# A hybrid decoder block on one core: 448 instead of 384 tokens of the expert mixer are gathered, the first value rows come beside the recurrence, and three transposes move behind the first dots

## The chip, the cores and the metric

The kernel runs on one core of one Trainium2 chip. The metric is the device time of one execution in microseconds (us), lower is better; one execution in each set is also recorded by the hardware profiler.

## What is computed

For 1024 tokens of width 1024 the block projects its modulated input, runs an RWKV-7 recurrence and a top-k attention beside each other, merges the two with gates, and then applies PEER, an expert mixer with product keys. PEER is the part that the change touches:

```python
# q, keys1, keys2: per head the 16 best of 128 keys on each side, then the 16 best of the 256 sums
idx  = i1 * 128 + i2                  # 8 heads x 16 slots = 128 experts of 16384 for every token
gate = softmax(scores)                # over the 16 slots of a head
h    = gelu(einsum('td,tkd->tk', h2, u[idx]))   # 128 dots of 1024 for a token
y    = einsum('tk,tkd->td', gate * h, v[idx])
out  = layer_norm(alpha * x + mod * y)
```

## The kernel before, in words

The projection, the recurrence and the attention run in two halves H of 512 tokens each (H=0, then H=1). In each half `rwkv` and `attn` are staggered, then `merge` writes what PEER needs. Beside `rwkv` of H=1 the first gathered rows of PEER are worked on, since the first half's tokens are known by then.

PEER is done in two ways, by token:

- **Gathered** (the first `NG` = 3 tiles of 128 tokens). For each of the 128 slots of a tile one indirect DMA fetches the u row that each token chose (128 partitions x 1024 floats, 0.524 MB), and VectorE takes its dot with the token (L1389). For each slot a second one fetches the v row, which VectorE multiplies by the gated dot and adds to the sum `pg` (L1391, L1393). The DMAs are issued by POOL (L1385, into tiles `g`, `gx`, `g2`). A "row" below is one such DMA with its VectorE operation: 256 for each tile, 768 in all, numbered from 0. Rows 0 to 7 have no due place; rows 8 to `ROW1` are tied to places in the recurrence of H=1 (56 "anchors" on VectorE, L699 and L763: the row's VectorE operation is placed no sooner than its anchor, `behind` at L1336); rows `EARLY` to `MIDDLE` go beside the table stage, the rest beside the dense stage. Rows below `EARLY` have three buffers (`g`, GB); between `EARLY` and `MIDDLE` three more (`gx`); after that `g` and one `g2`.
- **Dense** (the other `DN` = 640 tokens). All 128 blocks of u and all 128 of v (128 rows each) stream through TensorE for all these tokens. A block is loaded as `raw` by SP (L1267), rounded to `whi` by ACT (L232), and its rest `wlo` is taken by POOL (L1271, `split2`). `mm6` (L1281) then issues, for each of 8 chunks, six matmuls of 128 x `DN`/2 columns (L1284, L1286, L1288): 48 of 320 columns for a block. 69 of the u blocks are done ahead in the table stage (`dots_ahead`, into `dotD`), the others in `dense_u` (L1301); v blocks are in `dense_v` (L1319), whose last group of 8 is streamed twice, once for 384 and once for 256 columns, so 264 blocks are split in all. The gates of these tokens are first written out as tables over all experts (`gate_table`, L1240): 16 chunks of 8 tokens for each 128 tokens, each with two comparisons on VectorE and 8 matmuls in 16 passes of TensorE (L1258).

`retrieve` (L1118) finds keys and gates for a tile of tokens; `by_slot` (L1228) transposes them on TensorE (L1233) for the table. Tiles 1 to 3 are retrieved beside the merge of H=1, tiles 4 to 7 in the table stage. Tile 3 is the first dense one. `finish` (L1424) scales a gathered tile's sum, adds the residual and normalises (`out_rows`, L1400); `fin1` (L1445) does the same for dense tokens after the last group.

A tile scheduler fixes the order of the instructions on each engine when the program is built; on the chip each engine works through its own list in that order. POOL's list holds both the `wlo` splits and the issues of the gather DMAs; an issue whose buffer is not yet free holds whatever stands behind it.

## Time and profile before

| | us |
|---|---|
| three runs | 3740.57, 3749.42, 3751.53 (median 3749.42) |
| the profiled execution: its own time | 3743.65 |
| its span in the profile | 3741.9 |
| PE busy | 3505.2 (94%) |
| VectorE (DVE) busy | 2596.4 (69%) |
| POOL busy | 1981.3 (53%) |
| ACT busy | 1695.7 (45%) |
| mean granted TensorE clock | 0.967 of full speed |

The parts of the span, in order: projection, recurrence and attention of H=0, its merge (about 780 us), the recurrence of H=1 with the first gathered rows (1018 to 1440 us), its merge (to 1643), the table stage (1643 to 2380), the dense stage (2380 to 3593), and the last 149 us, in which the last 24 of the 264 blocks are split. PE is TensorE's matmuls, DVE is VectorE, ACT is ScalarE, POOL is GpSimd, SP is SyncE. The rows of the trace that the prediction uses stand in a section of their own below. A PE row with "x2" is two passes that the trace shows together; every shown time is from the start of the span.

### The profile page before, as it was taken

How to read it: one execution, taken by the hardware profiler on the slowest of the kernel's cores; microseconds unless marked ns; L12 is line 12 of the kernel's file. 1: busy time of each engine (PE TensorE's matmuls, PEld its weight loads, DVE VectorE, ACT ScalarE, POOL GpSimd, SP SyncE). 2: the span in 40 equal slices, each digit the busy share in tenths (PEclk: the TensorE clock that was granted, in tenths of full speed). 3: DMA queues.
4: the chain of work that ended last, by engine and by line, in shares of the span. 5: the costliest groups of instructions: out<-in, count | busy, mean ns of one | idle time of the engine just before them, and what ended most of it. 6: DMA issues, size and time to landing. Idle time of an engine off the chain costs nothing.

```text
span 3741.9 us, 64784 instructions
## 1 busy us (share of the span) xinstructions
PE 3505.2 (94%) x24045; PEld 3139.0 (84%) x24045; DVE 2596.4 (69%) x5433; ACT 1695.7 (45%) x3230; POOL 1981.3 (53%) x1572
## 2 busy tenths in 40 slices
PE   8999999889999999869999999999999999999997
PEld 7677777666677777649999989999999999999997
DVE  7756653857467775899999985376777767676754
ACT  3549953243344443447667678322223322222223
POOL 5452222354455553245655532467677667677755
PEclk9999999989999999889999999999999999999998
DMA  7463323864676666378988864898999989989963
GB/s 231 137 171 103 107 87 123 290 196 161 214 220 219 215 212 218 115 250 317 335 308 316 309 240 171 292 333 322 334 330 331 323 319 327 340 320 325 333 225 123
DMA packets 436880, 920.95 MB, mean 246 GB/s; under 512 B 36452, under 2 KB 195508, under 8 KB 433876
## 3 DMA queue, kind: packets, MB, share of 16 engines
q1 hardware_dynamic: 311956, 498.38, 39.8%
q0 software_dynamic: 124608, 418.43, 31.4%
q8 instruction: 189, 3.10, 0.3%
q14 instruction: 127, 1.04, 0.1%
HBM read 791.59 MB, written 125.08 MB: 245 GB/s over the span
## 4 chain that ended last, share of the span: by engine, by line
PE 49%; DVE 14%; DMA 13%; issue 8%; POOL 7%; ACT 6%; SPq 0%; POOLq 0%; ACTq 0%; DVEq 0%
PE pair L1284 7%; PE pair L1286 7%; PE pair L1288 7%; PE acc L423 4%; PE acc L424 4%; PE acc L425 4%; POOL g L1385 3%; DMA g<-in_u_dram,gidx 3%; DMA raw<-in_vt_dram 3%; POOL wlo L1271 3%; DMA g<-in_v_dram,gidx 3%; PE tp L1258 2%; DMA raw<-in_ut_dram 2%; ACT gt L232 2%; PE acc L975 2%
## 5 line engine op out<-in xcount | busy, mean ns | idle before, releaser
L1271 POOL TENSOR_TENSOR wlo<-raw,whi 128x1024 fp32r<-128x1024 f32 x264 | 643.8, 2440 | 388.9 <-ACT whi L232 367.5
L413 POOL TENSOR_TENSOR wlo<-wraw,whi 128x512 fp32r<-128x512 f32 x280 | 371.3, 1329 | 557.3 <-ACT whi L232 505.9
L232 ACT ACTIVATE whi<-raw 128x1024 fp32r<-128x1024 f32 x264 | 278.9, 1057 | 681.1 <-PE pair L1286 320.7
L1385 POOL DMA_INDIRECT g<-in_u_dram,gidx x361 | 373.6, 1035 | 298.4 <-DVE g L1389 180.5
L1284 PE MATMUL pair<-A,whi 128*128 128x320 f32 (+2 forms) x2048 | 482.1, 312 | 25.6 <-DVE A L1316 18.3
L1393 DVE SCALAR_TENSOR_TENSOR pg<-g,dots,pg 128x1024 f32<-128x1024 f32 x317 | 407.1, 1284 | 123.1 <-DMA g<-in_v_dram,gidx 118.0
L1286 PE MATMUL pair<-A,whi 128*128 128x320 f32 (+2 forms) x2048 | 481.2, 311 | 0.2 <-DVE A L1316 0.2
L1288 PE MATMUL pair<-A,wlo 128*128 128x320 f32 (+2 forms) x2048 | 480.4, 311 | 0.6 <-POOL wlo L1271 0.6
L1288 PE MATMUL pair<-h2T,wlo 128*128 128x320 f32 x2048 | 474.3, 312 | 2.1 <-POOL wlo L1271 2.1
L1284 PE MATMUL pair<-h2T,whi 128*128 128x320 f32 x2048 | 475.6, 312 | 0.2 <-ACT ds L232 0.2
L1286 PE MATMUL pair<-h2T,whi 128*128 128x320 f32 x2048 | 473.3, 311 | 0.0
L1385 POOL DMA_INDIRECT g<-in_v_dram,gidx x320 | 307.7, 961 | 170.8 <-DVE pg L1393 80.8
L423 PE MATMUL acc<-big,whi 128*128 128x512 f32 x864 | 356.5, 413 | 18.6 <-DVE zs L531 6.8
L1284 PEld LDWEIGHTS pair<-A,whi 128*128 128x128 f32 x2048 | 349.1, 190 | 28.2 <-issue 19.1
L1389 DVE SCALAR_TENSOR_TENSOR g<-g,pg 128x1024 f32<-128x1024 f32 x233 | 281.0, 1216 | 118.4 <-DMA g<-in_u_dram,gidx 116.8
L425 PE MATMUL acc<-big,wlo 128*128 128x512 f32 x864 | 351.6, 407 | 2.3 <-POOL wlo L413 2.3
L424 PE MATMUL acc<-big,whi 128*128 128x512 f32 x864 | 349.5, 404 | 3.1 <-DVE big L449 3.1
L1288 PEld LDWEIGHTS pair<-A,wlo 128*128 128x128 f32 x2048 | 349.1, 190 | 0.8 <-POOL wlo L1271 0.8
L1286 PEld LDWEIGHTS pair<-A,whi 128*128 128x128 f32 x2048 | 349.2, 190 | 0.7 <-DVE A L1316 0.7
L1288 PEld LDWEIGHTS pair<-h2T,wlo 128*128 128x128 f32 x2048 | 343.8, 189 | 3.5 <-POOL wlo L1271 2.6
L1284 PEld LDWEIGHTS pair<-h2T,whi 128*128 128x128 f32 x2048 | 344.6, 189 | 1.6 <-ACT ds L232 0.4
L1286 PEld LDWEIGHTS pair<-h2T,whi 128*128 128x128 f32 x2048 | 343.9, 189 | 1.0
(482 smaller groups left out, 6682.5 us busy)
## 6 DMA issues: line engine op xcount, KB each, us to landing
raw<-in_vt_dram SPq DMA_DIRECT2D x136, 512.0 KB
raw<-in_ut_dram SPq DMA_DIRECT2D x128, 512.0 KB
gtD<-st SPq DMA_DIRECT2D x20, 2048.0 KB
gt<-gtD SPq DMA_DIRECT2D x32, 1280.0 KB
wraw<-in_wz_dram SPq DMA_DIRECT2D x152, 256.0 KB
dotD<-ds SPq DMA_DIRECT2D x69, 320.0 KB
al<-dotD SPq DMA_DIRECT2D x69, 320.0 KB
mw<-in_wada_dram SPq DMA_DIRECT2D x32, 512.0 KB
```

The source lines that it names most:

```text
L232: copy = lambda o, i, **k: A.activation(o, i, AF.Copy, **k)
L413: G.tensor_tensor(lo, raw, hi.bitcast(F32), op=OP.subtract)
L423: mm(pt, lhsT=wh[:, ks], rhs=ah[:, k, :], start=k == 0, stop=False)
L424: mm(pt, lhsT=wh[:, ks], rhs=al[:, k, :], start=False, stop=False)
L425: ins = mm(pt, lhsT=wl[:, ks], rhs=ah[:, k, :], start=False, stop=k == nk - 1)
L1271: G.tensor_tensor(lo, raw, hi.bitcast(F32), op=OP.subtract)
L1284: mm(pts[n], lhsT=wh, rhs=ah[:, h], start=k == 0, stop=False)
L1286: mm(pts[n], lhsT=wh, rhs=al[:, h], start=False, stop=False)
L1288: mm(pts[n], lhsT=wl, rhs=ah[:, h], start=False, stop=last)
L1385: G.indirect_dma_start(out=u, out_offset=None, in_=a["u" if n < 2 else "v"], in_offset=bass.IndirectOffsetOnAxis(ap=idx[:, k:k + 1], axis=0))
L1389: V.scalar_tensor_tensor(u, u, 1.0, h2, op0=OP.mult, op1=OP.mult, accum_out=dots[:, k:k + 1])
L1393: V.scalar_tensor_tensor(acc, u, dots[:, k:k + 1], acc, op0=OP.mult, op1=OP.add)
```

## The change

A fourth, smaller tile of 64 tokens (`GX`) is gathered, so `DN` falls from 640 to 576 and a matmul of `mm6` from 320 to 288 columns; the last group is split 384 + 192. The small tile is packed: partitions 0 to 63 carry slots 0 to 63 of its 64 tokens, partitions 64 to 127 slots 64 to 127, so it takes 64 u rows and 64 v rows, each still 128 x 1024. Its two halves are added by two matmuls with a matrix `sel` in `finish`. Its index, gates and token rows come by two SP DMAs each (`rows_in`); one more tile of `xaD` and `h2D` is written in the merge of H=0 (one DVE and one POOL product of 128 x 1024 for each, two SP DMAs). The gate table of tile 3 has 8 chunks instead of 16.

Rows up to 192 instead of 128 are tied to the recurrence of H=1: the first tile's first 64 value rows are now among them. They are summed in SBUF (`gacc`) and copied once to PSUM at row 192. `MIDDLE` moves from 300 to 364, so that 172 rows stay beside the table stage. The name `GX` of before, the three extra buffers, is now `XR`.

Tile 3's `by_slots` (three transposes and the copies behind them) no longer stands ahead of the table stage: it comes after the first three blocks of dots (`FIRST`), tied behind the last matmul of the third.

```diff
-EARLY = 128
+EARLY = 192
...
-MIDDLE = 300
+MIDDLE = 364
...
-GX = 3
+FIRST = 3
+XR = 3
...
-ROW1 = 128
+ROW1 = 192
 NG = 3
-TD = NG * 128
+GX = 64
+TD = NG * 128 + GX
+NGT = NG + (GX > 0)
 DN = 1024 - TD
...
-        for tt, xn in enumerate(xns[:max(0, NG - 4 * H)]):
+        for tt, xn in enumerate(xns[:max(0, NGT - 4 * H)]):
...
-        for b in range(16):
+        for b in range(max(0, TD - i * 128) // 8, 16):
...
     def gather_all(at):
-        for i in range(NG):
+        for i in range(NGT):
             acc = yield from peer_gather(i, at)
             finish(i, acc, at)
+    def rows_in(dst, src, n, c):
+        for r in range(128 // n):
+            at = 0 if src.shape[1] == c else r * c
+            nc.sync.dma_start(dst[r * n:r * n + n, 0:c], src[0:n, at:at + c])
     def peer_gather(i, at):
         pg = at["pg"]
+        tokens = 128 if i < NG else GX
+        slots_ = tokens
+        halves = 2 if i < NG else 1
...
-        for n in range(4):
-            half = slice(64 * (n % 2), 64 * (n % 2) + 64)
-            if n == 2:
-                acc = pg.tile([128, 1024], F32, name="pg")
+        for n in range(2 * halves):
+            half = slice(0, slots_) if halves == 1 else slice(64 * (n % 2), 64 * (n % 2) + 64)
+            if n == halves:
+                acc = (gp.tile([128, 1024], F32, name="gacc") if i == 0 and EARLY > 128 else
+                       pg.tile([128, 1024], F32, name="pg"))
...
+                if row == EARLY and EARLY > 128:
+                    so_far, acc = acc, pg.tile([128, 1024], F32, name="pg")
+                    copy(acc, so_far)
...
     def finish(i, acc, at):
+            sel = gp.tile([128, 1024], F32, name="gh2")[:, 0:n]
+            V.tensor_reduce(sel, ident.rearrange("p (s t) -> p t s", t=n), axis=AX.X, op=OP.add)
+            copy(y2, acc)
+            acc = at["pg"].tile([128, 1024], F32, name="pg")
+            for h in range(2):
+                hs = slice(512 * h, 512 * h + 512)
+                mm(acc[p, hs], lhsT=sel, rhs=y2[:, hs], start=True, stop=True)
...
-                side = retrieve_all(range(1, M1), tk, by_slots)
+                side = retrieve_all(range(1, M1), tk, keep)
...
-            for i in slots:
-                table(i)
...
             ahead_ = dots_ahead()
+            for _ in range(FIRST):
+                next(ahead_)
+            for i, f in early_found.items():
+                with tc.issue_after(latest[0].ins):
+                    by_slots(i, f)
+                table(i)
```

In the built program there are 896 rows instead of 768; 169 instead of 118 of them stand between the first and the last anchor in the recurrence of H=1. In the line numbers of the changed kernel the row DMA is L1402, its products L1406 to L1410, `wlo` L1274, the matmuls of `mm6` L1287, L1289 and L1291, the transposes L1236, the end of a gathered tile L1432.

DVE's list in the recurrence of H=1, before (`ST` is the state, `w` a work tile of the recurrence, `g` a gathered row):

```order
L699 TENSOR_TENSOR w<-w,rw 128x256
L1389 SCALAR_TENSOR_TENSOR g,dots<-g,gh_15759 128x1024
L684 TENSOR_TENSOR w<-w,C 128x256
L763 TENSOR_TENSOR ST<-ST,fs 128x128
L1389 SCALAR_TENSOR_TENSOR g,dots<-g,gh_15759 128x1024 x2
L687 STREAM_TRANSPOSE in<-w 128x256 x2
```

and after:

```order
L760 TENSOR_TENSOR ST<-ST,rw 128x128
L1406 SCALAR_TENSOR_TENSOR g,dots<-g,gh_15768 128x1024
L690 STREAM_TRANSPOSE in<-w 128x256
L687 TENSOR_TENSOR w<-w,C 128x256
L960 ISA p,asm<-tp,mask_8226 128x512
L960 ISA asm 128x1
L766 TENSOR_TENSOR ST<-ST,fs 128x128
L1406 SCALAR_TENSOR_TENSOR g,dots<-g,gh_15768 128x1024
```

More rows stand between the same steps of the recurrence and the attention, 169 where there were 118.

PE's list at the start of the table stage, before (L425 is the last matmul of the merge, L1233 the transposes of tile 3, L1128 the keys of the next tile, L1284 and so on the first block of dots):

```order
L425 MATMUL acc<-Q,wlo 128x512
L1233 MATMUL tp<-ident,i_15675 128x128
L1233 MATMUL tp<-ident,gates 128x128
L1233 MATMUL tp<-ident,i_15674 128x128
L1128 MATMUL tp<-keysT,qT 128x128 x4
L1284 MATMUL pair<-h2T,whi 128x320 x2
```

and after, the end of the merge with the first dots:

```order
L428 MATMUL acc<-Q,wlo 128x512
L1287 MATMUL pair<-h2T,whi 128x288 x2
L1289 MATMUL pair<-h2T,whi 128x288 x2
L1287 MATMUL pair<-h2T,whi 128x288 x2
L1289 MATMUL pair<-h2T,whi 128x288 x2
```

and, three blocks of dots on, the place to which the transposes have moved:

```order
L1289 MATMUL pair<-h2T,whi 128x288 x2
L1291 MATMUL pair<-h2T,wlo 128x288 x2
L1236 MATMUL tp<-ident,i_15685 128x128
L1236 MATMUL tp<-ident,gates 128x128
L1236 MATMUL tp<-ident,i_15684 128x128
L1131 MATMUL tp<-keysT,qT 128x128 x2
```

The dots now stand ahead of the transposes on PE.

POOL's list at its end, before (`g` and `g_36500` are the last row DMAs, `wlo` the blocks' splits, L1415 the normalisation of dense rows):

```order
L1271 TENSOR_TENSOR wlo<-raw,whi 128x1024
L1385 DMA g<-in_v_dram,gidx 128x1024 x3
L1385 DMA g_36500<-in_v_dram,gidx 128x1024
L1271 TENSOR_TENSOR wlo<-raw,whi 128x1024 x11
L1415 TENSOR_TENSOR gacc<-gacc,gt 128x512 x2
L1271 TENSOR_TENSOR wlo<-raw,whi 128x1024 x6
```

and after, around the last `wlo` of the program, behind which only rows and the normalisation of the last tiles stand:

```order
L1402 DMA g_36486<-in_u_dram,gidx 128x1024
L1274 TENSOR_TENSOR wlo<-raw,whi 128x1024
L1402 DMA g<-in_u_dram,gidx 128x1024 x3
L1274 TENSOR_TENSOR wlo<-raw,whi 128x1024
L1402 DMA g_36498<-in_u_dram,gidx 128x1024
L1402 DMA g<-in_u_dram,gidx 128x1024 x3
L1402 DMA g_36510<-in_u_dram,gidx 128x1024
L1402 DMA g<-in_u_dram,gidx 128x1024 x3
```

Before, the last row stands ahead of the last 22 splits, and 7 rows stand behind the 240th. After, 137 rows stand behind the 240th split: 52 between it and the last one, and 85 (21 u rows and the 64 v rows of the small tile) behind the last one. Between the 72nd and the 240th split there were 461 rows, 2.74 for each; now there are 395, 2.35 for each.

## Rows read from the trace of the kernel before

**Rows 1.** Busy time by stretch: start:end, length, busy us (count), clock, DMA share, GB/s.

```profile
core 0: us, PE busy (x) PEld busy (x) DVE busy (x) ACT busy (x) POOL busy (x), PEclk, DMA share, GB/s
275.00:643.00 368.00, 354.80 (x3363) 278.92 (x3362) 199.36 (x575) 248.10 (x622) 96.91 (x101) 0.96 0.34 102
1018.00:1440.00 422.00, 388.88 (x3616) 303.54 (x3617) 299.04 (x669) 195.89 (x434) 221.62 (x192) 0.97 0.70 217
1643.00:1677.00 34.00, 2.99 (x16) 1.93 (x15) 28.79 (x64) 10.52 (x14) 19.26 (x17) 0.56 0.91 321
1677.00:2250.00 573.00, 548.13 (x3885) 534.66 (x3886) 523.76 (x1249) 397.23 (x811) 316.66 (x222) 0.99 0.83 300
1800.00:1900.00 100.00, 96.27 (x695) 94.49 (x694) 91.20 (x168) 70.48 (x149) 64.58 (x47) 0.98 0.94 349
2380.00:3593.00 1213.00, 1194.50 (x8073) 1192.10 (x8073) 851.97 (x1042) 340.24 (x419) 838.51 (x628) 0.99 0.91 327
3593.00:3742.00 149.00, 125.86 (x848) 124.72 (x846) 61.47 (x86) 43.14 (x55) 81.48 (x43) 0.93 0.41 138
```

**Rows 2.** The same by stretch, for line 1385 (row DMAs issued by POOL) alone.

```profile
1018.00:1440.00 422.00, 136.75 (x117) 0.97 0.70 217
2380.00:3593.00 1213.00, 435.14 (x461) 0.99 0.91 327
```

**Rows 3.** DVE's waits in the recurrence of H=1: total us, times, longest us.

```profile
DVE g L1389 <- DMA g<-in_u_dram,gidx: 40.4, 34, 3.2
```

**Rows 4.** One piece of the chain that ended last, in the recurrence: start, us.

```profile
1057.32 6.26 DMA g<-in_u_dram,gidx
```

**Rows 5.** Timeline of PE and POOL, start of the table stage: start, us, idle before.

```profile
1674.93 0.45 PE L1233 MATMUL tp<-ident,i 128*128 128x128 f32 x1 [31.01 <-DVE i L1193]
1676.89 0.90 PE L1284 MATMUL pair<-h2T,whi 128*128 128x320 f32 x2
1657.53 4.64 POOL L1271 TENSOR_TENSOR wlo<-raw,whi 128x1024 fp32r<-128x1024 f32 x2
```

**Rows 6.** Timeline of PE: matmuls of 320, 384 and 256 columns in a row.

```profile
2649.97 0.46 PE L1288 MATMUL pair<-h2T,wlo 128*128 128x320 f32 x2
2650.85 0.46 PE L1288 MATMUL pair<-h2T,wlo 128*128 128x320 f32 x2
3659.82 0.33 PE L1288 MATMUL pair<-A,wlo 128*128 128x384 f32 x1
3660.51 0.33 PE L1284 MATMUL pair<-A,whi 128*128 128x384 f32 x1
3702.05 0.29 PE L1284 MATMUL pair<-A,whi 128*128 128x256 f32 x1
3702.54 0.28 PE L1286 MATMUL pair<-A,whi 128*128 128x256 f32 x1
```

**Rows 7.** PE's costliest groups: the passes of the gate tables, busy us, mean ns.

```profile
L1258 PE MATMUL tp<-gt 128*128 128x128 f32 x1280 | 161.7, 279 | 14.2 <-ACT st L232 11.5 <-ACT sc L232 2.5
```

**Rows 8.** Timeline of DVE in the dense stage: first and last of eight products.

```profile
3126.79 1.22 DVE L1389 SCALAR_TENSOR_TENSOR g<-g,pg 128x1024 f32<-128x1024 f32 x1 [3.25 <-DMA g<-in_u_dram,gidx]
3142.36 1.22 DVE L1389 SCALAR_TENSOR_TENSOR g<-g,pg 128x1024 f32<-128x1024 f32 x1
```

**Rows 9.** Timeline of POOL: a split, two row DMAs in a row, the last split.

```profile
3593.11 2.42 POOL L1271 TENSOR_TENSOR wlo<-raw,whi 128x1024 fp32r<-128x1024 f32 x1 [8.85 <-ACT whi L232]
3596.93 0.94 POOL L1385 DMA_INDIRECT g<-in_v_dram,gidx  x1 [0.30 <-issue]
3598.18 0.94 POOL L1385 DMA_INDIRECT g<-in_v_dram,gidx  x1 [0.30 <-issue]
3716.94 4.75 POOL L1271 TENSOR_TENSOR wlo<-raw,whi 128x1024 fp32r<-128x1024 f32 x2 [2.32 <-ACT whi L232]
```

**Rows 10.** Timeline of POOL in the merge of H=0, and of DVE near the end.

```profile
783.39 8.58 POOL L1089 TENSOR_TENSOR xo<-xo,big 128x1024 f32<-128x1024 f32 x2
3725.76 0.48 DVE L1330 SCALAR_TENSOR_TENSOR yacc<-pair,modc,yacc 128x256 f32<-128x256 f32 x1 [2.15 <-PE pair L1288]
```

More of the change, by code (lines that the diff above doesn't have):

```diff
@@ L442, in body @@
         ybD[H] = tc.dram_tile([8, 128, 512], F32, name=f"ybD{H}")
-    xaD = [tc.dram_tile([128, 1024], F32, name=f"xaD{i}") for i in range(NG)]
-    h2D = [tc.dram_tile([128, 1024], F32, name=f"h2D{i}") for i in range(NG)]
+    xaD = [tc.dram_tile([128, 1024], F32, name=f"xaD{i}") for i in range(NGT)]
+    h2D = [tc.dram_tile([128, 1024], F32, name=f"h2D{i}") for i in range(NGT)]
     xaT = tc.dram_tile([128, 8, DN], F32, name="xaT")
@@ L1213, in retrieve @@
         V.tensor_tensor(gv, gv, gs[:, :, None].to_broadcast([128, 8, 16]), op=OP.mult)
-        if i < NG:
-            ef = i1
+        if i < NGT:
+            ef = i1 if i < NG else tp_.tile([128, 128], F32, name="ef")
             V.scalar_tensor_tensor(ef, i1, 128.0, i2, op0=OP.mult, op1=OP.add)
@@ L1287, in mm6 @@
         for n, h in enumerate(halves):
-            mm(pts[n], lhsT=wl, rhs=ah[:, h], start=False, stop=last)
+            latest[:] = [mm(pts[n], lhsT=wl, rhs=ah[:, h], start=False, stop=last)]
     def dots_u(i1, du, h2T, bufs):
@@ L1343, in gather_all @@
     def gather_all(at):
-        for i in range(NG):
+        for i in range(NGT):
             acc = yield from peer_gather(i, at)
             finish(i, acc, at)
+    def rows_in(dst, src, n, c):
+        for r in range(128 // n):
+            at = 0 if src.shape[1] == c else r * c
+            nc.sync.dma_start(dst[r * n:r * n + n, 0:c], src[0:n, at:at + c])
     def peer_gather(i, at):
         pg = at["pg"]
+        tokens = 128 if i < NG else GX
+        slots_ = tokens
+        halves = 2 if i < NG else 1
         def index(row):
             t = (gp if row < EARLY else at["du"] if row < MIDDLE else at["dv"]).tile([128, 128], U32, name="gidx")
-            nc.sync.dma_start(t, idxD[i])
+            rows_in(t, idxD[i], tokens, slots_)
             return t
         def room(row):
-            if EARLY <= row < MIDDLE and row % (GB + GX) >= GB:
-                return at["sl"].tile([128, 1024], F32, name="gx", bufs=GX)
+            if EARLY <= row < MIDDLE and row % (GB + XR) >= GB:
+                return at["sl"].tile([128, 1024], F32, name="gx", bufs=XR)
             if row >= MIDDLE and row % (GB + GM) >= GB:
@@ L1366, in peer_gather @@
         gates = gp.tile([128, 128], F32, name="ggate")
-        nc.sync.dma_start(gates, gateD[i])
+        rows_in(gates, gateD[i], tokens, slots_)
         h2 = gp.tile([128, 1024], F32, name="gh2")
-        nc.sync.dma_start(h2, h2D[i])
+        rows_in(h2, h2D[i], tokens, 1024)
         if i > 0:
@@ L1394, in peer_gather @@
                 yield
-            if n < 2:
+            if n < halves:
                 A.activation(dots[:, half], dots[:, half], AF.Gelu)
@@ L1424, in finish @@
     def finish(i, acc, at):
-        last = i == NG - 1
+        last = i == NGT - 1
+        n = 128 if i < NG else GX
+        p = slice(0, n)
         row, xa = ((at["dv"].tile([128, 2 * DN], F32, name="A", bufs=AB)[:, 0:1024] if last else grow()) for _ in range(2))
@@ L1429, in finish @@
         y2 = gp.tile([128, 1024], F32, name="gacc")
-        V.tensor_tensor(y2, acc, row, op=OP.mult)
-        nc.sync.dma_start(xa, xaD[i])
-        V.tensor_tensor(y2, y2, xa, op=OP.add)
+        if n == 128:
+            V.tensor_tensor(y2, acc, row, op=OP.mult)
+        else:
+            sel = gp.tile([128, 1024], F32, name="gh2")[:, 0:n]
[5 more added lines that the diff above has]
+                mm(acc[p, hs], lhsT=sel, rhs=y2[:, hs], start=True, stop=True)
+            V.tensor_tensor(y2[p], acc[p], row[p], op=OP.mult)
+        nc.sync.dma_start(xa[p], xaD[i][p])
+        V.tensor_tensor(y2[p], y2[p], xa[p], op=OP.add)
         g, b = at["ln"][0:2] if last else (grow(), grow())
@@ L1436, in finish @@
             rowb(b, "ln2b")
-        out_rows(i * 128, 128, (y2[:, 0:512], y2[:, 512:1024]), y2, g, b, gp.tile([128, 16], F32, name="lnst"), last)
+        out_rows(i * 128, n, (y2[:, 0:512], y2[:, 512:1024]), y2, g, b, gp.tile([128, 16], F32, name="lnst"), last)
     def fin_rows(du):
@@ L1462, in body @@
     slots = {}
+    early_found = {}
     def by_slots(i, f):
```

7 lines of the change are left out of this document (5 added, 2 removed).

## The prediction

> **What bounds the kernel now.** I read the busy time by stretch first, then the waits and the chain where two engines were close, then timelines for the price of a single step. In the dense stretch (2380 to 3593 us) PE is busy 1194.5 of 1213 us at a clock of 0.99 [rows 1]; its matmuls follow each other without a gap [rows 6]. It sets the pace there, while the DMA share of 0.91 and POOL's 838.5 us lie beside it. In the table stage (1677 to 2250) PE has 548 of 573 us and DVE 524 [rows 1]: two engines are close, and a gain on one shows only as far as the other lets it. At its start PE sits idle for 31 us, waiting for tile 3's DVE chain [rows 5]. In the recurrence of H=1 PE is idle 33 of 422 us, where the same stretch of H=0, without rows, leaves 13 of 368 [rows 1]; DVE waits 40.4 us for gathered rows [rows 3], and such a DMA is a piece of the chain [rows 4]. The last 149 us hold 24 splits and 7 rows: PE is busy 126 us and the DMA share falls to 0.41 [rows 1].
>
> The sum goes from the profiled execution's own time, 3743.65 us; it is 5.8 us under the median of the runs and inside their range. About 0.3% (11 us) is what a measurement of this kernel can tell from no change.
>
> **The change part by part.**
>
> 1. *The fourth output tile in the merge of H=0.* Two products on POOL take 8.58 us [rows 10] and two on DVE run beside; two SP DMAs join the queue ahead of the next loads. Hidden they cost 0, in line some 10 us. I take **+5**, half of the POOL row, since POOL also makes the merge's `wlo`.
>
> 2. *The recurrence of H=1 with 169 rows instead of 118.* DVE gets 51 more operations of about 1.3 us (1.22 and a read of the accumulator), 66 us, where it is busy 299 of 422 us [rows 1]. The row DMAs have three buffers here. One takes 6.26 us to land [rows 4], 1.3 for the product and 0.3 until the next issue [rows 9]: 7.9 us for three, 2.6 us for a row; 118 rows need 307 us of the 422, but 169 need 439. So the ring becomes the pace of the stretch: +17. Rows already cost something at the smaller number: 20 us more PE idle than in H=0 for 118 rows, 0.17 each, which makes 9 to 29 us for 51 to 169 of them. Bounds: +9, if the DMAs land sooner when more are asked for, and +83, if the whole of DVE's work lies in line beside the ring. I take **+30**: the ring's 17 and half of the other, since DVE's list is in order and a late row holds the recurrence behind it. The cost on POOL, 51 issues of some 1.2 us [rows 2], has room (222 of 422 us busy). The v rows' sum in SBUF and its one copy are below 2 us and in that bound.
>
> 3. *The late transposes and the table stage.* Three blocks of dots need `whi` and `wlo`, and POOL makes the first `wlo` from 1657.5 to 1662 [rows 5]. So dots can start at about 1661 instead of 1676.9: 16 us of the idle 31. The chain from DVE's `i` to the first table gets no shorter, but the tables' transposes have three blocks (some 20 us) of other work ahead of them. In the stage 69 blocks x 48 matmuls become shorter. A matmul of 320 columns takes 0.88 us / 6 = 147 ns, one of 384 takes 0.69 / 4 = 173, one of 256 takes 0.49 / 4 = 123 [rows 6]; at 288 that is about 133, so 13.4 ns less: 3312 x 13.4 = 44 us. The 8 chunks of table that go are 128 of 1280 passes, 128 x 0.126 = 16 us of PE [rows 7]. PE loses 76 us in all. But DVE is busy 91 of 100 us in the middle of the stage [rows 1], the 172 rows beside it stay, and of its work only 16 comparisons go. Bounds: -20 (the start and little more) and -76. I take **-45**, midway, as both engines are equally near their limit.
>
> 4. *The dense stage up to the 240th split.* 59 blocks of dots and 120 of values are 179 x 48 = 8592 matmuls; x 13.4 ns = 115 us less. Rows per split fall from 2.74 to 2.35. The moved bytes are 327 GB/s x 7.2 us = 2.36 MB for a split now, of which rows are 1.44 and the block 0.52; afterwards rows take 1.23, the rest some 0.88: 2.11 MB in 6.6 us, or 320 GB/s, which is about what runs now [rows 1, 2]. So the DMA engines don't stop it. I take 12 us off for waits that were hidden by longer matmuls: **-103**; bounds -50 and -120.
>
>    The Trainium skill ("TensorE: Matmul & The Clock Gate", "Back-to-back issue gap") has 81 ns for a sustained matmul of 128 columns and 131 ns for one of 512, so 0.13 ns for a column. By that 32 columns would save only 4.2 ns, 36 us here and 14 in the table stage; the rows at 256, 320 and 384 columns lie 0.4 ns for a column apart, and the sum goes by them.
>
> 5. *The end.* Now 149 us pass from the 240th split to the end of the span. Afterwards 24 splits and 52 rows come first. PE needs for them 8 blocks of 48 matmuls at 133 ns, 8 of 24 at 173 and 8 of 24 at 98 (192 columns, by the slope between 256 and 320): 51 + 33 + 19 = 103 us; POOL needs 24 x 2.42 + 52 x 1.25 = 123 us (a row DMA follows the other in 1.25 us) [rows 9]. I take 128, what they take now up to the last split. Then **85 rows stand behind the last split** with nothing beside them. Price of one: at least POOL's 1.25 us [rows 9]; the eight fastest in the trace, with four buffers, came in 15.57 / 8 = 1.95 us [rows 8], beside other loads; 0.524 MB at 349 GB/s, the fastest 100 us that I cite [rows 1], is 1.50. I take 1.75, between the last two, as the loads are gone: 149 us. From the last dense sum to the end are 16 us now [rows 10]; a tile's end, with the two matmuls that add its halves, 18. Together 128 + 149 + 18 = 295: **+146**; bounds +103 (1.25 each) and +163 (1.95).
>
> Sum: 5 + 30 - 45 - 103 + 146 = +33, or 3776.7 against the own time, 3782 against the median; I write 3780.
>
> **The rivals.**
>
> *PE alone sets the pace up to the last split (faster).* Then the recurrence gives only its +9, the start and the table stage the full -76, the dense stage -115: 5 + 9 - 76 - 115 + 146 = -31, some 3713. For it: PE is over 92% busy in all three stretches. Against it: DVE's 91% in the table stage and the ring in the recurrence. It decides for faster from the point where these stretches together give over 162 us, the +146 of the end, the 5, and the 11 that can be told apart; my own terms give 118.
>
> *The rows at the end run at POOL's issue pace (no change).* With 1.25 us for each of the 85, 43 us less than I take: -10, 3734. For it: no other transfer is left, and four buffers at 1.25 us allow 5 us for a turn. Against it: 0.524 MB in 1.25 us is 419 GB/s, more than any stretch of the trace moved [rows 1]. The Trainium skill ("DMA: Bandwidth & Descriptors", the anatomy of a gpsimd DMA) gives about 2.0 us and the bytes at 436 GB/s for one such DMA, which would be 3.2 us and speak for this rival; the trace's row in the recurrence took 6.26 us to land.
>
> *The static order costs more than I take (slower).* If the recurrence pays the full +83, or if the dense stage gives only 50 because splits stand behind row DMAs whose buffer isn't free, the sum is about +86: 3830.
>
> *Columns hardly count (slower).* If a matmul's price went with the quoted gap, the dense stage would give 36 - 12 and the table stage 20: 5 + 30 - 20 - 24 + 146 = +137, 3881. The rows at three widths speak against it.
>
> *The change doesn't do what it says.* The early dots could wait as long as the transposes did, if their tokens' tiles come late: POOL issues those loads right before the first `wlo`. That takes back up to 16 us, inside the range of the forecast.
>
> **How the numbers follow.** The forecast (slower, 3755 to 3815) has 0.44; PE alone 0.22; the issue pace at the end 0.12; the costly order 0.10; columns 0.02. Mixtures of a cheap end and a cheap recurrence that land within the bound, 0.05; mixtures a little above the forecast, 0.05. So faster 0.22, same 0.12 + 0.05 = 0.17, slower 0.44 + 0.10 + 0.02 + 0.05 = 0.61. The range runs from 3712 (PE alone) to 3835 (the costly order) and leaves out some 0.2: columns, and the far ends of the two rivals. The forecast's own range is 3755 to 3815, as signs of both kinds carry weight.
>
> **What would show it.** The recurrence of H=1 should take about 450 us and DVE's wait for gathered rows should rise well over 40.4; the PE idle at the start of the table stage should fall to about 15; the dense stretch up to the 240th split should be near 1110 us; and behind the last split there should be some 150 us in which PE is idle and the DMA share stays high. The forecast is wrong if that last stretch is below 110 us, or if the recurrence takes less than 435 us together with a table stage over 60 us shorter.

## The result, and the profile after

The changed kernel took 3855.52 us (median of 4 runs, 3849.62 to 3865.65), the kernel before 3750.48 (4 runs): a ratio of 1.0284, interval 1.0257 to 1.0311. It is slower, as forecast, but by 105 us where some 30 were forecast. The profiled executions took 3849.62 and 3743.65 us, and their spans differ by 105.9.

The busy time by stretch of the changed kernel, cut at the corresponding events ([rows 1] end the table stage early, at 2250, and begin the dense stage 5 us late; recurrence, its merge, the wait for the first dots, table stage, dense stage to the 240th split, the last 24 splits, and what stands behind them):

```profile
core 0: us, PE busy (x) PEld busy (x) DVE busy (x) ACT busy (x) POOL busy (x), PEclk, DMA share, GB/s
1024.00:1506.00 482.00, 408.05 (x3618) 317.10 (x3612) 366.59 (x719) 200.51 (x437) 273.96 (x241) 0.91 0.78 244
1506.00:1729.00 223.00, 189.91 (x820) 144.90 (x820) 181.67 (x711) 89.62 (x159) 84.92 (x67) 0.93 0.59 190
1729.00:1741.00 12.00, 0.43 (x2) 0.43 (x3) 11.50 (x60) 6.30 (x8) 6.01 (x9) 0.69 0.94 287
1741.00:2420.00 679.00, 629.12 (x4663) 612.83 (x4663) 572.50 (x1365) 461.77 (x933) 359.12 (x244) 0.96 0.79 287
2420.00:3519.00 1099.00, 1083.41 (x8067) 1080.61 (x8066) 745.87 (x911) 329.95 (x421) 776.02 (x564) 0.99 0.91 327
3519.00:3670.00 151.00, 129.92 (x867) 126.89 (x866) 105.90 (x161) 41.72 (x49) 116.00 (x82) 0.92 0.87 303
3670.00:3848.00 178.00, 7.46 (x36) 4.10 (x34) 123.23 (x135) 9.13 (x13) 88.42 (x91) 0.52 0.76 257
```

and four stretches of the kernel before that [rows 1] do not have, the merge of H=1, the table stage and the dense stage in full, and the last 24 splits:

```profile
1439.00:1644.00 205.00, 186.06 (x809) 141.79 (x807) 159.60 (x720) 89.47 (x156) 67.98 (x52) 0.93 0.54 169
1677.00:2375.00 698.00, 672.00 (x4789) 658.02 (x4790) 569.68 (x1294) 491.28 (x1003) 351.24 (x235) 0.99 0.78 282
2375.00:3593.00 1218.00, 1199.50 (x8108) 1197.10 (x8107) 853.62 (x1044) 343.29 (x423) 840.92 (x629) 0.99 0.91 327
3593.00:3722.00 129.00, 121.05 (x809) 120.14 (x808) 52.55 (x70) 39.87 (x49) 75.21 (x39) 0.97 0.45 152
```

From event to event the two spans add up so (us). A stretch "to the 72nd split" ends where 72 splits are done and the next one starts, and so for the 240th:

| stretch | before | after | difference | my term |
|---|---|---|---|---|
| up to the recurrence of H=1 | 1017.6 | 1024.5 | +6.9 | +5 |
| recurrence of H=1 | 421.3 | 481.9 | +60.6 | +30 |
| merge of H=1 | 205.0 | 222.5 | +17.5 | none |
| wait for the first dots, and the table stage to the 72nd split | 731.2 | 691.2 | -40.0 | -45 |
| dense stage, from there to the 240th split | 1218.0 | 1098.9 | -119.1 | -103 |
| last 24 splits | 128.6 | 151.0 | +22.4 | +146 with the next row |
| behind the last split | 20.2 | 177.8 | +157.6 | in the row above |

The gains came near the forecast. PE's first dots wait 12 us where the transposes waited 31 [rows 5], and a matmul of 288 columns takes (2651.19 - 2649.72) / 11 = 133.6 ns (133 forecast):

```profile
1740.57 0.85 PE L1287 MATMUL pair<-h2T,whi 128*128 128x288 f32 x2 [11.66 <-ACT whi L235]
...
2649.72 0.30 PE L1287 MATMUL pair<-A,whi 128*128 128x288 f32 x1
2651.19 0.29 PE L1287 MATMUL pair<-A,whi 128*128 128x288 f32 x1
```

What the gains were spent on is DVE in the recurrence and the ring of buffers at the end. DVE's waits for gathered rows in the recurrence, which were 40.4 us [rows 3], and POOL's waits behind the last split (total us, times, longest; the answers are cut, marked by dots):

```profile
DVE g L1406 <- DMA g<-in_u_dram,gidx: 49.1, 48, 3.6
DVE gacc L1410 <- DMA g<-in_v_dram,gidx: 25.6, 21, 4.1
...
POOL g L1402 <- DVE pg L1410: 39.3, 46, 1.5
POOL g L1402 <- DVE g L1406: 9.5, 12, 2.3
```

In the recurrence DVE is busy 68 us longer, at almost the same idle time (422 - 299 = 123 before, 482 - 367 = 115 after), so by this trace alone the stretch grew by about what DVE was given; the experiments show that the fetches have a share in it as well. The granted clock was lower where PE had more gaps (0.97 with 33 us of them, 0.91 with 74), and PE is busy 408 instead of 389 us with the same matmuls. Behind the last split PE is all but idle and POOL waits 58 times, 48.8 us in all, for a product to free a buffer (85 rows are issued there).

### The profile page after: what moved, and what is told of

It is laid out like the page before. It is cut to its first block, busy times and chain, and to the rows that moved or that the text cites. A ratio compares the mean times of both kernels' runs of the same rounds, so it can differ in the third digit from the quotient of the medians.

```text
span 3847.8 us, 65009 instructions
## 1 busy us (share of the span) xinstructions
PE 3383.9 (88%) x23921; PEld 3001.6 (78%) x23921; DVE 2740.4 (71%) x5625; ACT 1659.8 (43%) x3162; POOL 2108.0 (55%) x1702
## 4 chain that ended last, share of the span: by engine, by line
PE 30%; DMA 13%; DVE 12%; issue 7%; POOL 6%; ACT 6%; SPq 0%; POOLq 0%; ACTq 0%; DVEq 0%
PE pair L1287 8%; PE pair L1291 8%; PE pair L1289 7%; DMA g<-in_v_dram,gidx 5%; DMA g<-in_u_dram,gidx 4%; ACT gt L235 3%; POOL g L1402 3%; POOL wlo L1274 2%; DMA raw<-in_ut_dram 2%; DVE g L1406 2%; PE tp L1261 1%; DVE pg L1410 1%; PE acc L978 1%; PE acc L426 1%; PE acc L428 1%
## 5 line engine op out<-in xcount | busy, mean ns | idle before, releaser
L1274 POOL TENSOR_TENSOR wlo<-raw,whi 128x1024 fp32r<-128x1024 f32 x264 | 637.4, 2416 | 318.4 <-ACT whi L235 313.3
L1402 POOL DMA_INDIRECT g<-in_u_dram,gidx x394 | 404.1, 1026 | 303.2 <-DVE g L1406 170.8
L1410 DVE SCALAR_TENSOR_TENSOR pg<-g,dots,pg 128x1024 f32<-128x1024 f32 x350 | 449.8, 1285 | 161.0 <-DMA g<-in_v_dram,gidx 152.0
L1402 POOL DMA_INDIRECT g<-in_v_dram,gidx x417 | 405.9, 973 | 256.3 <-DVE pg L1410 89.5
L1287 PE MATMUL pair<-A,whi 128*128 128x288 f32 (+2 forms) x2048 | 457.4, 300 | 27.5 <-DVE A L1319 13.9
L1287 PE MATMUL pair<-h2T,whi 128*128 128x288 f32 x2048 | 450.2, 300 | 21.0 <-ACT whi L235 15.7
L1291 PE MATMUL pair<-h2T,wlo 128*128 128x288 f32 x2048 | 449.3, 300 | 14.1 <-POOL wlo L1274 14.1
L1289 PE MATMUL pair<-A,whi 128*128 128x288 f32 (+2 forms) x2048 | 456.2, 299 | 4.0 <-DVE A L1319 4.0
L1291 PE MATMUL pair<-A,wlo 128*128 128x288 f32 (+2 forms) x2048 | 455.8, 299 | 2.4 <-POOL wlo L1274 2.3
L1289 PE MATMUL pair<-h2T,whi 128*128 128x288 f32 x2048 | 449.6, 300 | 0.0
L1406 DVE SCALAR_TENSOR_TENSOR g<-g,pg 128x1024 f32<-128x1024 f32 x266 | 320.0, 1214 | 104.6 <-DMA g<-in_u_dram,gidx 103.5
L1287 PEld LDWEIGHTS pair<-A,whi 128*128 128x128 f32 x2048 | 339.4, 192 | 30.4 <-issue 14.3
L1287 PEld LDWEIGHTS pair<-h2T,whi 128*128 128x128 f32 x2048 | 335.1, 191 | 23.5 <-ACT whi L235 16.3
L1291 PEld LDWEIGHTS pair<-h2T,wlo 128*128 128x128 f32 x2048 | 334.4, 191 | 17.7 <-POOL wlo L1274 16.9
L1289 PEld LDWEIGHTS pair<-A,whi 128*128 128x128 f32 x2048 | 339.5, 192 | 4.8 <-DVE A L1319 4.8
L1291 PEld LDWEIGHTS pair<-A,wlo 128*128 128x128 f32 x2048 | 339.3, 192 | 3.3 <-POOL wlo L1274 3.3
L1289 PEld LDWEIGHTS pair<-h2T,whi 128*128 128x128 f32 x2048 | 335.5, 191 | 1.0
```

The source lines that it names most:

```text
L1274: G.tensor_tensor(lo, raw, hi.bitcast(F32), op=OP.subtract)
L1287: mm(pts[n], lhsT=wh, rhs=ah[:, h], start=k == 0, stop=False)
L1289: mm(pts[n], lhsT=wh, rhs=al[:, h], start=False, stop=False)
L1291: latest[:] = [mm(pts[n], lhsT=wl, rhs=ah[:, h], start=False, stop=last)]
L1402: G.indirect_dma_start(out=u, out_offset=None, in_=a["u" if n < halves else "v"], in_offset=bass.IndirectOffsetOnAxis(ap=idx[:, k:k + 1], ...
L1406: V.scalar_tensor_tensor(u, u, 1.0, h2, op0=OP.mult, op1=OP.mult, accum_out=dots[:, k:k + 1])
```

## The experiments

**Parts alone and parts taken out.** Four kernels undo or do one part each.

The late transposes undone:

```diff
-FIRST = 3
+FIRST = 0
-                side = retrieve_all(range(1, M1), tk, keep)
+                side = retrieve_all(range(1, M1), tk, by_slots)
...
+            for i in slots:
+                table(i)
             side = retrieve_all(range(M1, 8), tk, table)
```

> The changed kernel with tile 3's transposes back at the start of the table stage (the other parts stay). Theory (the late transposes give PE some 20 us there, as the traces show: first dots 64 us later than before where the merge ends 85 us later): PE sits idle about 31 us at the start again and the time rises by 15 to 20 us, to about 3873. Rival (the table stage is bound by DVE or by the table chain, so the gain is given back inside the stage): within 5 us of the changed kernel's 3855.

Measured: 3866.4 us, 1.0295 (1.0266 to 1.0324), against 1.0284 of the changed kernel. In its trace PE waits 36 us between the merge and the first dots where the changed kernel waits 12, but that profiled execution lies 23 us above its own median, and the two ratios differ by 0.0011, some 4 us, within their intervals. By itself it does not decide.

The late transposes alone, in the kernel before (`GX = 0`, `EARLY` and `ROW1` 128, `MIDDLE` 300, `FIRST` 3):

> The kernel before with the late transposes alone. Theory: 16 to 20 us of PE idle at the start of the table stage go and stay gone: 3731 to 3735. Rival (given back inside the table stage, where DVE is busy 91%): 3750, within 5 us of before.

Measured: 3741.13 us (12 runs) against 3754.24, 0.9967 (0.9951 to 0.9984): faster by 12 us, a little under the theory's 16 to 20. The 31 us of idle PE [rows 5] are down to 13, and the stretch from the merge to the 72nd split is 16 us shorter (715.1 against 731.2). What the first dots wait for now is the load of their tokens:

```profile
1661.74 0.87 PE L1287 MATMUL pair<-h2T,whi 128*128 128x320 f32 x2 [12.96 <-DMA h2T<-h2TD]
```

This part is worth keeping: the kernel is faster than the kernel before and the changed kernel.

The early value rows taken out:

```diff
-EARLY = 192
+EARLY = 128
-MIDDLE = 364
+MIDDLE = 300
-ROW1 = 192
+ROW1 = 128
```

> The changed kernel without the early value rows (EARLY and ROW1 128, MIDDLE 300). The recurrence of H=1 holds 118 rows again, and 143 instead of 85 rows stand behind the last split. Theory (both ends are bound by rows: 1.2 us for each early one by the traces, 1.9 for each late one): recurrence and merge 78 us shorter, the end 58 x 1.9 = 110 us longer, so about 3885. Rival (the early rows are what made the kernel slow, and rows behind the last split run at POOL's 1.25 us): 3855 - 78 + 72 = 3849 or less.

Measured: 3914.77 us, 1.0434 (1.0403 to 1.0465). The recurrence is back at 426 us and the merge at 207, 72 us less than in the changed kernel, but 143 rows stand behind the last split and take 300 us with the closing. So the early rows are cheaper where they are than at the end; the rival falls, and the theory's 3885 was still too low: the end cost 122 us more, not 110, recurrence and merge gave 72, not 78, and the table and the dense stage, which the theory left out, took 10 us more each (701 and 1108 us).

The early value rows alone (`GX = 0`, old transposes, `EARLY` 192):

> The kernel before with the early value rows alone (640 dense tokens, no small tile, old transposes). Theory: the recurrence and the merge of H=1 cost 78 us more, and nothing comes back, since PE bounds the dense stage: 3820 to 3830. Rival (64 rows less beside the dense stage relieve its DMA, which runs at a share of 0.91): dense 20 to 60 us shorter, 3770 to 3810.

Measured: 3820.7 us, 1.0182 (1.0153 to 1.0212). The recurrence takes 485 us and the merge 230; the dense stage from the 72nd to the 240th split gives back 15.5 us of it (1202.5 against 1218.0). The theory holds: 64 rows less beside the dense stage are worth little, as PE sets the pace there.

**The end: is it the ring?** Rows from 811 on go to the `A` tiles, twelve buffers that the dense stage no longer needs:

```diff
         def room(row):
+            if row >= 811:
+                return at["dv"].tile([128, 2 * DN], F32, name="A", bufs=AB)[:, 0:1024]
```

> The changed kernel with twelve more buffers for the last 85 rows (row 811 and on go into the tiles of A, which the dense stage no longer needs there; in the built order 81 rows then stand behind the last split). Theory (the four buffers' turn-around sets 1.86 us a row behind the last split, where POOL waited 48 us for products to free a buffer): a row takes 1.25 to 1.55 us, the stretch behind the last split falls from 178 to 120 to 145 us, and the kernel to 3800 to 3825. Rival (the DMA engines, busy 0.86 there, or VectorE's 1.3 us for a product set the pace): 170 us or more, within 10 us of 3855.

Measured: 3821.95 us, 1.0203 (1.0165 to 1.0242), some 30 us below the changed kernel; the stretch behind the last split is 138 us instead of 178, as the theory had it. The issues now stand one behind the other at 1.25 us, and the DMA moves 403 GB/s (busy time by stretch, the same 90 us in 40 slices, then POOL's timeline):

```profile
3690.00:3780.00 90.00, 0.00 (x0) 0.00 (x0) 86.93 (x96) 4.79 (x8) 69.50 (x73) 0.50 1.01 403
...
GB/s 348 397 428 415 424 417 421 422 413 428 417 415 399 246 264 304 344 395 417 422 417 419 426 417 421 415 419 421 417 424 417 421 422 417 424 417 421 419 421 419
...
3722.70 0.94 POOL L1404 DMA_INDIRECT A<-in_v_dram,gidx  x1 [0.30 <-issue]
3723.94 0.94 POOL L1404 DMA_INDIRECT A<-in_v_dram,gidx  x1 [0.30 <-issue]
3725.19 0.94 POOL L1404 DMA_INDIRECT A<-in_v_dram,gidx  x1 [0.30 <-issue]
```

In the changed kernel the same list reads as follows, with one product of VectorE among its issues:

```profile
3740.30 0.94 POOL L1402 DMA_INDIRECT g<-in_v_dram,gidx  x1 [0.57 <-DVE pg L1410]
3742.45 0.94 POOL L1402 DMA_INDIRECT g<-in_v_dram,gidx  x1 [1.22 <-DVE pg L1410]
3744.35 0.94 POOL L1402 DMA_INDIRECT g<-in_v_dram,gidx  x1 [0.96 <-DVE pg L1410]
...
3746.00 1.29 DVE L1410 SCALAR_TENSOR_TENSOR pg<-g,dots,pg 128x1024 f32<-128x1024 f32 x1 [0.60 <-DMA g<-in_v_dram,gidx]
3747.56 0.94 POOL L1402 DMA_INDIRECT g<-in_v_dram,gidx  x1 [0.95 <-DVE pg L1410]
```

The turn of one buffer can be followed there: it is issued at 3740.30, the row's product waits for the landing and starts at 3746.00, and the buffer is issued again at 3747.56. That is 7.26 us, and over four buffers 1.81 us a row. So four buffers set the pace of the 85 rows: an issue follows the other by 1.81 us on average, and by 1.31 once there are more buffers. Neither the DMA engines nor VectorE held them at 1.81. With twelve buffers three limits lie together: POOL's issues at 1.25 us, a DMA share of 1.01, and VectorE, busy 86.9 of 90 us.

**The recurrence: product or fetch?** Two theories were put against each other. First only on the 64 value rows: not fetched (the products read the token's tile), or fetched with products of 8 columns, or neither.

```diff
+                bare = n >= halves and row < EARLY
-                u = room(row)
+                u = h2 if bare else room(row)
-                G.indirect_dma_start(
+                bare or G.indirect_dma_start(
...
+                        w = slice(0, 8 if row < EARLY else 1024)
-                        V.scalar_tensor_tensor(acc, u, dots[:, k:k + 1], acc, op0=OP.mult, op1=OP.add)
+                        V.scalar_tensor_tensor(acc[:, w], u[:, w], dots[:, k:k + 1], acc[:, w], op0=OP.mult, op1=OP.add)
```

> The changed kernel in which the 64 early value rows (128 to 191) are not fetched: their products read the token's own tile instead, so VectorE has the same work and the ring of three buffers carries 118 rows again in the recurrence of H=1 (the first tile's output is not the reference's). Theory A (VectorE's products lie in line with the recurrence, 1.29 us each): the recurrence stays at 470 to 482 us. Theory B (the ring of three buffers is the pace): it falls to 420 to 445.

> The changed kernel in which the 64 early value rows are fetched, but their products take 8 of 1024 columns (the rest of the first tile's output is left out). Theory A (VectorE's work is the price): the recurrence of H=1 falls from 482 to 425 to 440 us. Theory B (the ring of three buffers and its DMAs): it stays at 460 to 482.

> The changed kernel in which the early value rows (128 to 191) are neither fetched nor multiplied in full: 64 products of 8 columns stay where the rows stood (the rest of the first tile's output is left out). Without fetching alone the recurrence of H=1 took 497 us, with 8 columns alone 469, against 482 in the changed kernel and 421 before. Theory C (each is enough: VectorE's list is in order, so the recurrence is held either by the product or by the wait for the row's DMA): with neither it falls to 415 to 440 us. Rival D (it is the order in which the recurrence and the attention now stand between the rows, not the rows' work): it stays at 455 to 485.

Measured for the recurrence of H=1, in one run of each kernel: 497 us without the fetch, 469 with thin products, 459 with neither; 482 in the changed kernel. No theory had forecast all three, and 455 to 485 for the last was the rival's. One reason is in the design: the value rows stand in the last third of the recurrence only, while the u rows, which nothing changed, are now packed into the first two thirds. Cut at the 20th and 38th anchor, the three thirds take (us, and rows in each):

| kernel | first | second | third |
|---|---|---|---|
| before | 139 (38) | 141 (41) | 141 (39) |
| changed | 164 (56) | 160 (57) | 158 (56) |
| value rows not fetched | 167 (56) | 166 (59) | 164 (66) |
| value rows with thin products | 166 (56) | 165 (57) | 137 (56) |
| neither | 171 (56) | 163 (59) | 125 (66) |

Where nothing was altered, 56 rows cost 20 to 30 us a third more than 39. The altered third can't be read alone: where the value rows are not fetched it holds ten rows more, and the scheduler moved other work across the last anchor (the merge has 820 matmuls in the changed kernel, 736 without the fetch, 857 with thin products, 863 with neither). Recurrence and merge together, from the recurrence's start to the merge's last matmul, hold the same work in all kernels: 704 us in the changed kernel, 699 without the fetch, 694 with thin products, 679 with neither, and 633 in the run without early values, where the 64 rows are not there. So 64 rows that neither fetch nor multiply much still leave 46 us, about what the first two thirds pay for 113 rows instead of 79. Whether they pay it for the rows' work or for the order in which recurrence and attention now stand between the rows, rival D, these three kernels don't tell. The next ones are read over both stretches, too.

**All 192 rows.** None fetched, all products full on a tile that stays; then all fetched and all products thin; then a kernel with no rows in the recurrence (`GX = 0`, late transposes, `EARLY` and `ROW1` 8, `MIDDLE` 180):

> The changed kernel in which none of the first 192 rows is fetched: their products read one tile that stays in SBUF and are of full size (the first tile's output is not the reference's). Theory A (VectorE's products are the price of a row in the recurrence): 455 to 490 us for the recurrence of H=1, against 482 in the changed kernel and 421 to 430 with 118 rows. Theory B (the ring of three buffers and the row's landing are the price): 385 to 425.

> The changed kernel in which all of the first 192 rows are fetched, but each product takes 8 of 1024 columns (the rest of the first tile's sums is left out). Theory A: the recurrence falls to 385 to 430 us. Theory B: it stays at 455 to 490, by the ring of 2.6 us a row.

> The kernel before with the late transposes and no rows tied to the recurrence (EARLY and ROW1 8). It gives the recurrence of H=1 without rows. Theory A (0.5 to 0.6 us a row up to 118, more behind it): 365 to 385 us. Rival E (the price is the same 1.2 us from the first row on): 290 to 345, which the PE time of 355 in H=0 speaks against. Rival F (up to 118 rows are free, H=1 is longer by its attention): 405 to 425.

Measured, recurrence alone: 447, 362 and 308 us, in one run of each kernel (3786.91, 3802.13 and 3869.33 us in all; the last has 78 rows behind its last split). Recurrence and merge of H=1 together, busy time by stretch, first before and after:

```profile
1018.00:1644.00 626.00, 573.94 (x4419) 444.51 (x4419) 457.63 (x1386) 285.36 (x590) 289.60 (x244) 0.96 0.65 201
```

```profile
1024.00:1729.00 705.00, 597.96 (x4438) 462.00 (x4432) 548.26 (x1429) 290.13 (x595) 358.88 (x308) 0.92 0.72 227
```

then nothing fetched, thin products, and no rows:

```profile
1023.00:1665.00 642.00, 578.87 (x4421) 450.49 (x4420) 537.25 (x1436) 287.92 (x592) 175.85 (x127) 0.94 0.34 101
```

```profile
1024.00:1678.00 654.00, 587.51 (x4439) 456.18 (x4434) 346.35 (x1421) 288.35 (x595) 316.33 (x309) 0.94 0.77 244
```

```profile
1015.00:1603.00 588.00, 559.35 (x4420) 435.75 (x4419) 300.64 (x1126) 282.20 (x590) 145.99 (x127) 0.99 0.36 109
```

Products alone cost 642 - 588 = 54 us, fetches alone 654 - 588 = 66, and both 705 - 588 = 117, nearly their sum. So neither theory stands alone: VectorE's list is in order, and the recurrence behind a row waits both for the row to land and for its product. With thin products VectorE waits 175 us for rows in the two stretches:

```profile
DVE g L1407 <- DMA g<-in_u_dram,gidx: 107.3, 68, 5.4
DVE gacc L1412 <- DMA g<-in_v_dram,gidx: 67.7, 44, 4.8
```

It also gives the price of a row by their number: the some 120 rows of the kernel before cost 626 - 588 = 38 us in the two stretches, 0.3 each; the 64 that the change adds cost 79 more, 1.2 each. With the late transposes on both sides, as in the kernel without rows, it is 636 - 588 = 48 us, 0.4 each, and 69 more, 1.1 each. Removing the 64 rows from the changed kernel gives 705 - 633 = 72, also 1.1 each. The granted clock goes the same way, 0.99, 0.96, 0.92. Other kernels with the early value rows took 708 to 724, so 705 is no outlier, and such a difference is good to some 10 us.

Two things stay open. No run gave the recurrence more than three buffers, so how much of the fetches' 66 us is the ring of buffers and how much the landing itself is not known. And the scheduler's order differs from kernel to kernel, so its share in the price of the added rows is not shown.

**Elsewhere than in the recurrence?** The early value rows tied to the merge of H=1 (`ROW1` 128, `EARLY` 192 in the changed kernel):

> The changed kernel with the early value rows tied to the merge of H=1 instead of the recurrence (ROW1 128, EARLY 192). The merge takes 205 us before, with VectorE busy 160 and 169 GB/s, so it has room for some 35 to 55 rows. Theory (a row costs where VectorE's list is the latency of the stage, less where PE streams): the recurrence returns to 420 to 430 us, the merge grows from 223 to 235 to 260; the kernel at 3800 to 3840. Rival (the rows cost the same wherever they stand before the table stage): 3845 to 3865.

Measured: 3856.55 us, 1.0284 (1.0254 to 1.0314). The recurrence is back at 427 us and the merge takes 259 instead of 223, 19 us less together, but 25 us more pass from there to the 72nd split: nothing is won, as the rival had it.

With the late transposes in the kernel before, 32 rows were moved to the end of the dense stage (`EARLY` and `ROW1` 96, `MIDDLE` 268), or to the merge (`ROW1` 96, `EARLY` 128):

> The kernel before with the late transposes and fewer rows in the recurrence of H=1: EARLY and ROW1 96 instead of 128, MIDDLE 268, so that 32 rows move to the end of the dense stage, where 7 rows stood behind the 240th split and the DMA share was 0.45. Theory (a row costs the recurrence 0.5 to 1.2 us, and the last splits have room for it): recurrence and merge 15 to 35 us shorter, the end the same; 3705 to 3725. Rival (rows cost little up to 118, where the ring isn't full, and the dense stage slows): 3735 to 3750.

> The kernel before with the late transposes and with rows 96 to 127 tied to the merge of H=1 instead of the recurrence (ROW1 96, EARLY 128). With 32 rows less the recurrence took 20 us less in the run with EARLY 96 (411 against 430). Theory (the merge takes 32 rows for little, as its DMA and VectorE have room): 10 to 20 us below the late transposes alone, so 3715 to 3732. Rival (the merge pays what the recurrence saves): 3735 to 3750.

Measured: 3756.58 us, 1.0027 (1.0008 to 1.0046), and 3783.77, 1.0092 (1.0070 to 1.0114), where the late transposes alone had 0.9967. The recurrence falls to 410 us in both, from 430, but part of that is other work which the scheduler moved into the merge (866 and 865 matmuls there, 808 with the late transposes alone). Recurrence and merge together take 629 us in the first and 667 in the second, against 636. So taking 32 rows out is worth 6.5 us, 0.2 each, and the dense stage (9 us more) and the last 24 splits (13 more) take more than that; standing in the merge, the 32 rows cost 37 us, 1.2 each. Both theories fall, and both times passed the rivals' 3735 to 3750 as well: the merge has room by its shares, and none in its order.

**The last 24 splits.** The twelve buffers from row 759 on, which leaves 28 rows there instead of 52; and all rows from 759 on tied behind the last split:

```diff
+            if row >= 759:
+                return at["dv"].tile([128, 2 * DN], F32, name="A", bufs=AB)[:, 0:1024]
...
-        G.tensor_tensor(lo, raw, hi.bitcast(F32), op=OP.subtract)
+        split[:] = [G.tensor_tensor(lo, raw, hi.bitcast(F32), op=OP.subtract)]
...
+                with tc.issue_after(split[0].ins) if row >= 759 else nullcontext():
                     G.indirect_dma_start(
```

> The changed kernel with the twelve more buffers from row 759 on; in the built order 28 rows stand between the 240th and the last split instead of 52, and 109 behind it. Theory (POOL, busy 116 of 151 us there with 24 splits and 52 row DMAs of 1.2 us, holds the splits, and PE waits): the stretch of the last 24 splits falls from 151 to 128 to 140 us, and a row behind the last split stays at 1.3 us, so that stretch is 109 x 1.3 + 25 = 165 us; the whole 3810 to 3835. Rival (the stretch is held by the raw loads, not by POOL): 145 to 152 us for the last 24 splits all the same.

> The changed kernel with the twelve more buffers, and all rows from 759 on behind the last split, so that none stands among the last 24 splits (52 there now, 28 with the buffers alone: 151 and 146 us). Theory (rows and the end of the third tile delay the splits and the normalisation of the dense rows by their work on POOL and VectorE): the last 24 splits take 122 to 135 us, as in the kernel before (129). Rival (it is the block's own loads or the narrower matmuls): 142 to 152. Behind them 137 rows at 1.3 us and the end of two tiles: 195 to 215 us.

Measured: 3860.34 us in one run with 28 rows, where the last 24 splits take 146 us; 3870.03 in one run with none, where they take 122:

```profile
3516.00:3638.00 122.00, 115.69 (x829) 115.08 (x828) 36.28 (x56) 37.98 (x46) 65.64 (x30) 0.97 0.42 137
3638.00:3868.00 230.00, 8.75 (x48) 5.29 (x47) 190.73 (x238) 10.23 (x15) 137.56 (x144) 0.52 0.84 325
```

So rows, with the end of the third tile, make the difference between 122 and 151 us, and narrower matmuls do gain there (129 before); raw loads, the rival, do not hold the stretch. But 28 rows gain nothing that can be told: other kernels with 51 to 56 rows there took 146 to 152 us. A simple price on POOL does not give that. Behind the last split both forecasts were too low, 184 us for 165 and 230 for 195 to 215, and the first kernel's 3860 missed its 3810 to 3835. In the changed kernel PE's gaps there are spread over five causes (the largest 8 us, for the normalisation of dense rows), and the clock is 0.92 against 0.97. Which of the rows' effects leads is left open.

## Why the prediction failed, by its steps

The sign was right, and so was it that the rows behind the last split would take more than the dense stage gives. The time lies above the range (3712 to 3835). Taking its steps in turn:

1. *The fourth output tile*, +5: +6.9 in the profiled execution; in other kernels with the same tile the recurrence starts between 1017 and 1025 us, in those without it between 1013 and 1020, so a few us are all that can be said.

2. *The recurrence*, +30, bounds +9 to +83: +60.6. This is the first step that failed, by its size. I took the ring as the pace and "half of the other". The ring's +17 rested on one landing of 6.26 us [rows 4]; the six longest in the recurrence's part of that chain run from 4.61 to 6.70, 5.8 on average, and with 5.8 the ring would need some 417 us for 169 rows and not pass the 422. The runs show instead that fetch and product add nearly in full, each some 0.3 us a row over all 192 rows, and that each of the 64 added rows costs 1.1 to 1.2 us over recurrence and merge, not the 0.17 that the first 118 seemed to cost. That 0.17 came from setting H=1 beside H=0; set beside H=1 without rows, the existing ones already cost 0.3 to 0.4 each. The merge is 17.5 us longer, and I had no term for it. 15 rows stand in it instead of one, and with the 64 value rows taken out it is back at 207; but with neither fetch nor full product it still takes 220, with two rows in it and 43 more matmuls, so what lengthens it is not shown. Together the two stretches cost 78 us, near the bound of +83, in which the whole of DVE's work lies in line beside the ring.

3. *Late transposes and table stage*, -45: -40.0. Right in the sum; the first dots came 21 us sooner behind the merge (16 forecast), and alone the late transposes are worth 12 us. The rest of the stage gave only 19 us, although columns and chunks were to take 60 us off PE: PE is busy 43 us less, at a clock of 0.96 instead of 0.99, and its gaps grew from 26 to 50 us. The forecast's reason, that DVE is as near its limit, fits (570 us busy before, 573 after), but no run tested it; taking a value midway between the bounds was a choice that came out.

4. *The dense stage*, -103: -119.1, right in kind. My count was wrong: 179 blocks, of which 8 are counted a second time among the last 24 splits; from the 72nd to the 240th split stand 168, and 8064 matmuls give 108 us at 13.4 ns, not 115. The 12 us that I took off were not lost. What goes beyond 108 lies mostly at the cut: the trace has some 40 matmuls more in that stretch before than after, about 6 us, and PE's gaps are 3 us shorter. The rule that was quoted beside it (Trainium skill, "TensorE: Matmul & The Clock Gate", "Back-to-back issue gap") would have given 36 us; the trace disagrees, with 133.6 ns at 288 columns against 147 at 320.

5. *The end*, +146, bounds +103 to +163: +180. Two parts. For the last 24 splits I took the 128 us of before, although POOL alone needed 123 there by my own count; they took 151. And a row behind the last split cost 1.81 us from issue to issue, close to the 1.75 that was taken: 152 us for 85, plus 25 to close instead of 18. What sets it is the turn of four buffers, 7.26 us. The 1.75 had been put between a rate of bytes and the spacing of products in the dense stage (in [rows 8] the two rows are the first and the ninth product), without working out that turn, so that its size came close is partly luck.

The rivals: "PE alone sets the pace" fell: PE has 74 us of gaps in the recurrence, where VectorE's list and the rows hold it. "The rows at the end run at POOL's issue pace" did not happen with four buffers, but its price is nearly reached with twelve (1.31 us a row), and my reason against it was wrong: 419 GB/s was called more than any stretch moved, and with more buffers the same rows move 403, and 413 to 428 in most of the slices. The Trainium skill ("HBM Reference", "Specifications (TRN2)") says that a core streaming alone measures about 425 GB/s; these slices agree. "The static order costs more than I take" was the nearest, at 0.10 and 3830: its first half, the full +83, is what came, once the merge is counted with the recurrence; its second half, a dense stage that gives only 50, did not. "Columns hardly count" fell by the 133.6 ns, and "the change doesn't do what it says" by the first dots, which wait 12 us. Neither of the two signs that were named for a wrong forecast came up: both looked for a kernel faster than forecast, and the miss lay on the other side.

Put together: +31 in the recurrence, +17.5 in the merge and +34 at the end were missed, 16 in the dense stage were too little, and the two small terms add 7: 73 us, the difference between +106 and +33.

## What to carry to other kernels

Moving work onto a stretch with idle time on every engine is not free when the stretch is a chain and the engine's list is in order: each piece is paid in line, and here the price of a piece rose from 0.3 or 0.4 to over 1.1 us with their number, so measure the stretch with none, with some and with more before adding. Count what an in-order queue still holds behind the last unit of the bounding engine, and price it by the turn of its buffers (landing, product, issue, divided by the buffers), not by bandwidth. Where a stage leaves its tiles free at the end, use them as buffers there: that was worth some 30 us here, though the kernel stayed slower than the one before (1.0203). And write signs of being wrong for both directions.

## What was not expected of the hardware

Row gathers of 0.524 MB ran at 403 GB/s, one each 1.31 us on average, when next to nothing else moved and twelve buffers stood ready; the fastest 100 us cited of the kernel before had 349. And gaps on PE went with a lower clock: in the recurrence and its merge the same matmuls were busy 559 us without rows, with 29 us of gaps and a granted clock of 0.99; 574 us in the kernel before, with 52 and 0.96; and 598 us in the changed kernel, with 107 and 0.92.
